# Ten of twelve products in Strassen form, and branch outputs kept in HBM

## The chip, the cores and the metric

The kernel runs on one core of a Trainium2 chip. The metric is the device time of one execution in microseconds (us). The kernel before took 1085.91 us, the median of three runs (1085.72 to 1088.47).

## The reference

One layer on a sequence of 1024 tokens with 1024 channels, all in float32:

```python
h = rmsnorm(x, norm_g)
u_a, v_a, z_a, x_b, c_b, b_b, z_b, g_a, g_b = split(h @ w_in, 9 segments of 1024)
u, v = gelu(u_a), rmsnorm(gelu(v_a), v_norm_g)
y_a = u * (tril(w_s[g]) @ v per 128-token chunk and group + b[g]) * silu(z_a)
y_b = b_b * causal_conv3(c_b * x_b) * silu(z_b)
merged = sigmoid(g_a) * (y_a @ w_branch_a) + sigmoid(g_b) * (y_b @ w_branch_b)
out = rmsnorm(x + merged @ w_out, final_norm_g)
```

There are twelve products of 1024 by 1024 by 1024: nine projections of h, one for each branch (called pa and pb), and the output projection (po).

## The kernel before

Each float32 operand is split into a high and a low part: ScalarE casts the value to the high part and VectorE subtracts it from the value for the low part (`split`, L67 to L69). One float32 product of a 128-row step is then three matmuls into the same PSUM bank, high with high, low with high, high with low (`mm`, L71 to L74). The transposed activations h stay in SBUF for the whole kernel (hT), as two parts of 4 MB.

`block` computes 128 output channels for all 1024 tokens: two halves of 512 tokens, eight steps over the contraction, three matmuls each, 48 matmuls of 128x512 in all. Its weights are one DMA of 512 KB (L265), one cast and one subtraction of 128x1024. A product is eight such blocks, 384 matmuls.

The stages follow each other: a start written out by hand (norm and transposes of x, L112 to L125), v with tokens on partitions, in two halves of 512 channels; branch A, per group of 128 channels the blocks pu and pz and the spatial matmuls pm (L298); gate ga and product pa by turns; branch B, per group the blocks pbc, pbx, pbb, pbz; gate gb and product pb by turns; and the output projection po with the final norm. Results of branches, gates and merged sums stay in SBUF, in 28 slots of 4 KB per partition.

Outside the start, a scheduler fixes the order of each engine's instructions at build time; on the chip each engine runs its list in that order. All loads are on SyncE's queue (SP), also in that order: a DMA there that waits for a semaphore holds back those behind it. A DMA also waits for the earlier one on its completion counter, of which there are eight (DMAHW0 to DMAHW7 in the listings).

Of the kernel before, what the change touches and what calls it, by code (L numbers as in the profile page):

```python
# [19 lines left out]
def hybrid_block(ctx: ExitStack, tc: tile.TileContext, x, norm_g, w_in, v_norm_g, w_spatial,  # L20
# [50 lines left out]
    def mm(acc, a, b, k, nk):  # L71
        """acc += a.T @ b to float32's accuracy; a and b are (high, low) parts."""
        for n, (i, j) in enumerate(((0, 0), (1, 0), (0, 1))):
            nc.tensor.matmul(acc, a[i], b[j], start=k == 0 and n == 0, stop=k == nk - 1 and n == 2)  # L74

    def row_bcast(name, ap):
        t = slot(name)
        nc.sync.dma_start(t, ap.to_broadcast([P, D]))
        return t

    hT = (hpool.tile([P, KT, S], F32R, tag="hT_hi", name="hT_hi"),
          hpool.tile([P, KT, S], F32R, tag="hT_lo", name="hT_lo"))
# [8 lines left out]
    def load_rows(w, k, c0, name):
        raw = wraw.tile([P, D], F32, tag="raw", name=name + "_raw")
        nc.sync.dma_start(raw, w[k * P:(k + 1) * P, c0:c0 + D])
        hl = pair(name)
        split(hl[0], hl[1], raw)
        return hl

    def load_half_rows(w, k, c0, name):
        """Rows k and k+1 (in 128s) of 512 columns."""
        raw = wraw.tile([P, 2, NH], F32, tag="raw", name=name + "_raw")  # L100
        nc.sync.dma_start(raw, w[k * P:(k + 2) * P, c0:c0 + NH].rearrange("(j p) e -> p j e", p=P))
        return raw

    def split_half_rows(raw, name):
        hi, lo = (t.rearrange("p (j e) -> p j e", j=2) for t in pair(name))
        split(hi, lo, raw)
        return [(hi[:, j, :], lo[:, j, :]) for j in range(2)]
# [17 lines left out]
    def v_mm(i, pv, w, k0, k1):  # L125
        ts_ = slice(i * P, (i + 1) * P)
        for k in range(k0, k1):
            mm(pv, [h[:, k, ts_] for h in hT], w[k], k, KT)

    def v_norm(i, vt):  # L130
        sq = small.tile([P, D], BF16, tag="junk", name=f"vsq{i}", bufs=1)
        ss = small.tile([P, 1], F32, tag="ss", name=f"vss{i}")
        nc.scalar.activation(sq, vt, AF.Square, accum_out=ss)
        r = rsqrt_mean([ss], f"rv{i}")
        for g in range(G):
            gs = slice(g * P, (g + 1) * P)
            nc.vector.scalar_tensor_tensor(vg[g][:, i * P:(i + 1) * P], vt[:, gs], r, gv_bc[:, gs],
                                           ALU.mult, ALU.mult)
# [292 lines left out]
```

## Time and profile before

| | before |
|---|---|
| median of three runs | 1085.91 us |
| span of the profiled execution | 1084.3 us |
| TensorE busy | 1075.3 us (99%) |
| VectorE busy | 320.5 us (30%) |
| ScalarE busy | 247.6 us (23%) |
| GpSimd busy | 27.5 us (3%) |
| read from HBM, written | 60.83 MB, 4.19 MB |

A profile is one execution. Its span is measured from the first to the last event of the core; it is 1.6 us below the median. The chain of waits goes back from the last instruction to what released it at each step. A row of the chain or the timeline is: start in us, duration in us, engine, names (tiles) and line. A row of an engine's instructions by line has busy us and the mean ns of one behind the bar, then the idle time ahead of them and what ended it.

### The profile page before, as it was taken

The page shows a single profiled execution, that of the slowest core. Times are in us where ns is not written, and L with a number is a line of the kernel's source. Part 1 is how long each engine was busy: PE and PEld are TensorE (multiplying, and loading weights), DVE is VectorE, ACT ScalarE, POOL GpSimd, SP SyncE. Part 2 cuts the span into 40 slices and gives each one's busy share as a digit, 9 for nine tenths or more (in the row PEclk, how much of TensorE's full clock was granted, in tenths as well). Part 3 has the DMA queues.
Part 4 walks back from the last instruction along what each step waited for, and adds up shares of the span by engine and source line. Part 5 has one row for each costly group of instructions (what it writes and reads, how often), then busy time and mean ns, then how long its engine had stood idle before and what let it go on. Part 6 is the DMA issues. An engine that isn't in the chain of part 4 may idle for free.

```text
span 1084.3 us, 11075 instructions
## 1 busy us (share of the span) xinstructions
PE 1075.3 (99%) x4850; PEld 892.1 (82%) x4850; DVE 320.5 (30%) x354; ACT 247.6 (23%) x297; POOL 27.5 (3%) x69
## 2 busy tenths in 40 slices
PE   8999999999999999999999999999999999999997
PEld 6888888888888888888888888888888888888886
DVE  5543322223311121113323233133231222138322
ACT  5533223323211111112120211111203111134212
POOL 3111000000000000000000000000000000000101
PEclk9999999999999999999999999999999999999999
DMA  7031111111111212121212121212121211114322
GB/s 291 27 106 44 39 39 39 54 44 39 49 49 40 59 39 59 39 59 39 59 39 59 39 59 40 59 39 59 39 59 39 59 40 58 39 59 155 111 84 78
DMA packets 92838, 65.74 MB, mean 61 GB/s; under 512 B 2141, under 2 KB 85109, under 8 KB 92790
## 3 DMA queue, kind: packets, MB, share of 16 engines
q1 hardware_dynamic: 91638, 62.94, 18.8%
q10 hardware_dynamic: 1152, 2.10, 0.7%
q8 instruction: 38, 0.62, 0.2%
q14 instruction: 10, 0.08, 0.0%
HBM read 60.83 MB, written 4.19 MB: 60 GB/s over the span
## 4 chain that ended last, share of the span: by engine, by line
PE 98%; DVE 1%; DMA 1%; ACT 0%; issue 0%; POOL 0%; SPq 0%; POOLq 0%; DVEq 0%; ACTq 0%
PE po L74 8%; PE pu L74 8%; PE pga L74 8%; PE pb L74 8%; PE pgb L74 8%; PE pbz L74 8%; PE pbb L74 8%; PE pbc L74 8%; PE pa L74 8%; PE pz L74 8%; PE pbx L74 8%; PE pv L74 7%; PE pm L298 1%; DMA xt<-in_x_dram 1%; PE xp L122 1%; DVE wv_lo L162 0%
## 5 line engine op out<-in xcount | busy, mean ns | idle before, releaser
L74 PE MATMUL po<-wo_hi,mT_lo 128*128 128x512 f32 (+1 forms) x136 | 51.2, 377 | 0.0
L74 PE MATMUL po<-wo_lo,mT_hi 128*128 128x512 f32 (+1 forms) x136 | 51.2, 376 | 0.0
L74 PE MATMUL po<-wo_hi,mT_hi 128*128 128x512 f32 (+1 forms) x136 | 51.2, 376 | 0.0
L74 PE MATMUL pu<-hT_hi,pu_hi 128*128 128x512 f32 x128 | 50.4, 394 | 0.0
L74 PE MATMUL pga<-hT_hi,pga_hi 128*128 128x512 f32 x128 | 49.9, 390 | 0.0
L74 PE MATMUL pu<-hT_hi,pu_lo 128*128 128x512 f32 x128 | 49.8, 389 | 0.0
L74 PE MATMUL pu<-hT_lo,pu_hi 128*128 128x512 f32 x128 | 49.8, 389 | 0.0
L74 PE MATMUL pga<-hT_hi,pga_lo 128*128 128x512 f32 x128 | 49.8, 389 | 0.0
L74 PE MATMUL pga<-hT_lo,pga_hi 128*128 128x512 f32 x128 | 49.8, 389 | 0.0
L74 PE MATMUL pz<-hT_hi,pz_hi 128*128 128x512 f32 x128 | 49.8, 389 | 0.0
L74 PE MATMUL pz<-hT_hi,pz_lo 128*128 128x512 f32 x128 | 49.8, 389 | 0.0
L74 PE MATMUL pz<-hT_lo,pz_hi 128*128 128x512 f32 x128 | 49.8, 389 | 0.0
L74 PE MATMUL pa<-ya_hi,pa_hi 128*128 128x512 f32 x128 | 49.8, 389 | 0.0
L74 PE MATMUL pa<-ya_hi,pa_lo 128*128 128x512 f32 x128 | 49.8, 389 | 0.0
L74 PE MATMUL pa<-ya_lo,pa_hi 128*128 128x512 f32 x128 | 49.8, 389 | 0.0
L74 PE MATMUL pbc<-hT_hi,pbc_hi 128*128 128x512 f32 x128 | 49.8, 389 | 0.0
L74 PE MATMUL pbc<-hT_hi,pbc_lo 128*128 128x512 f32 x128 | 49.8, 389 | 0.0
L74 PE MATMUL pbc<-hT_lo,pbc_hi 128*128 128x512 f32 x128 | 49.8, 389 | 0.0
L74 PE MATMUL pbx<-hT_hi,pbx_hi 128*128 128x512 f32 x128 | 49.8, 389 | 0.0
L74 PE MATMUL pbx<-hT_hi,pbx_lo 128*128 128x512 f32 x128 | 49.8, 389 | 0.0
L74 PE MATMUL pbx<-hT_lo,pbx_hi 128*128 128x512 f32 x128 | 49.8, 389 | 0.0
L74 PE MATMUL pbb<-hT_hi,pbb_hi 128*128 128x512 f32 x128 | 49.8, 389 | 0.0
(217 smaller groups left out, 2239.7 us busy)
## 6 DMA issues: line engine op xcount, KB each, us to landing
xt<-in_x_dram SPq DMA_DIRECT2D x15, 512.0 KB, 6.5
wv_raw<-in_w_in_dram SPq DMA_DIRECT2D x8, 512.0 KB, 7.9
pu_raw<-in_w_in_dram SPq DMA_DIRECT2D x8, 512.0 KB, 3.6
pz_raw<-in_w_in_dram SPq DMA_DIRECT2D x8, 512.0 KB, 3.6
pga_raw<-in_w_in_dram SPq DMA_DIRECT2D x8, 512.0 KB, 3.6
pa_raw<-in_w_branch_a_dram SPq DMA_DIRECT2D x8, 512.0 KB, 3.9
pbc_raw<-in_w_in_dram SPq DMA_DIRECT2D x8, 512.0 KB, 3.6
pbx_raw<-in_w_in_dram SPq DMA_DIRECT2D x8, 512.0 KB, 3.6
```

The source lines that it names most:

```text
L74: nc.tensor.matmul(acc, a[i], b[j], start=k == 0 and n == 0, stop=k == nk - 1 and n == 2)
L122: nc.tensor.transpose(pt[:, k * P:(k + 1) * P], xt[:, ds_], ident)
L298: nc.tensor.matmul(pm[:, ns], vg[g][:, ns], wsT[:, g * P:(g + 1) * P], start=True, stop=True)
```

## The change

Ten of the twelve products (all but v and the output projection) go in Strassen's form as Winograd arranged it. `step` computes two blocks of 128 output channels at a time, which lie 512 channels apart, for all tokens. Both operands are seen as two by two blocks of halves; eight products of halves become seven, each four steps over the contraction of 512 tokens, so 12 matmuls. A step is 84 matmuls, and there are four steps for each product, 40 in all. The sums of blocks of h (T1 to T4) are made once, and those of weights (S1 to S4) in each step, by VectorE. The seven products accumulate in three PSUM banks (px, pe, pz): products 1, 3, 5 and 7 all add to px, and between them ScalarE copies or VectorE adds the running sum into the result tile C. The last partial sum stays in px.

- Tiles: 20 tiles of 8 KB per partition (`big`), 10 of 4 KB (`page`), two for raw loads (`rawt`); 8 PSUM banks of 512.
- h is kept as four blocks of halves instead of hT. VectorE copies each transposed tile once more from PSUM, and that copy goes to HBM (h_d); `h_blocks` loads halves back in v's second half and makes T1, T2, T4, T3 from them through the two raw tiles.
- v goes to HBM (v_d) without its norm; branch A loads it per group and multiplies the norm in (L437).
- Branch B now comes ahead of branch A, then all of ga, all of gb, then all of pa, and all of pb. What a branch gives goes to HBM as seven blocks, the sums among them (`keep_y`), and is loaded and split again as operand of pa or pb (`y_blocks`). Gates (g_d), the product pa times its gate (ta_d), and the merged sums (m_d) pass through HBM too.
- The output projection loads m per tile of 128 tokens and splits it there. The last pb block is no longer done by halves of the tokens.

```diff
-    NSLOT = 28
+    HP = KT // 2
...
-    hpool = ctx.enter_context(tc.tile_pool(name="hpool", bufs=1))
-    wraw = ctx.enter_context(tc.tile_pool(name="wraw", bufs=3))
-    wspl = ctx.enter_context(tc.tile_pool(name="wspl", bufs=2))
-    slots = ctx.enter_context(tc.tile_pool(name="slots", bufs=NSLOT))
-    ps = ctx.enter_context(tc.tile_pool(name="ps", bufs=3, space=bass.MemoryType.PSUM))
-    ps1 = ctx.enter_context(tc.tile_pool(name="ps1", bufs=2, space=bass.MemoryType.PSUM))
...
+    tp = ctx.enter_context(tc.tile_pool(name="tp", bufs=20))
+    pp = ctx.enter_context(tc.tile_pool(name="pp", bufs=10))
+    rp = ctx.enter_context(tc.tile_pool(name="rp", bufs=2))
+    ps = ctx.enter_context(tc.tile_pool(name="ps", bufs=8, space=bass.MemoryType.PSUM))
+    dp = ctx.enter_context(tc.tile_pool(name="dp", bufs=1, space=bass.MemoryType.DRAM))
...
-    def transpose_x(i, xt, bank=psum1):
-        ts_ = slice(i * P, (i + 1) * P)
-        for k0 in range(0, KT, 4):
...
+    def transpose_x(i, xt):
+        cs = slice(i % 4 * P, (i % 4 + 1) * P)
+        st = page(f"hst{i}").rearrange("p (k t) -> p k t", k=KT)
+        for kh in range(2):
...
-            split(hT[0][:, k0:k0 + 4, ts_], hT[1][:, k0:k0 + 4, ts_], pt.rearrange("p (k t) -> p k t", k=4))
...
+            src = block4(pt)
+            hi, lo = B[kh][i // 4]
+            split(hi[:, :, cs], lo[:, :, cs], src)
+            nc.vector.tensor_copy(st[:, kh * HP:(kh + 1) * HP, :], src)
+        nc.sync.dma_start(h_d[:, :, i * P:(i + 1) * P], st)
...
+    def v_out(i, h, pv):
+        vt = page(f"v{h}_{i}")[:, :NH]
+        nc.scalar.activation(vt, pv, AF.Gelu)
+        sq = small.tile([P, NH], BF16, tag="junk", name=f"vsq{h}_{i}", bufs=1)
+        nc.scalar.activation(sq, vt, AF.Square, accum_out=vss[:, 2 * i + h:2 * i + h + 1])
+        nc.sync.dma_start(v_d[i * P:(i + 1) * P, halves[h]], vt)
...
+    def h_raw(kh, th):
+        t = block4(rawt(f"h{kh}{th}"))
+        nc.sync.dma_start(t, h_d[:, kh * HP:(kh + 1) * HP, halves[th]])
...
+    def h_blocks(n):
+        if n == 0:
+            a, b = h_raw(0, 0), h_raw(0, 1)
+            tt_halves(a, b, a, ALU.subtract)
+            T["T1"] = t_block("T1", a)
+            c = h_raw(1, 1)
+            tt_halves(a, c, a, ALU.subtract)
+            T["T2"] = t_block("T2", a)
+            d = h_raw(1, 0)
+            tt_halves(d, d, a, ALU.subtract)
+            T["T4"] = t_block("T4", d)
+        else:
+            a, b = h_raw(1, 1), h_raw(0, 1)
+            tt_halves(a, a, b, ALU.subtract)
+            T["T3"] = t_block("T3", a)
...
+        if i == 1:
+            h_blocks(0)
+        if i == 4:
+            h_blocks(1)
...
+    def weights(w, c0, name):
+        raw = rawt(name + "_raw").rearrange("p (b k e) -> p b k e", b=2, k=KT)
+        for b in range(2):
+            nc.sync.dma_start(raw[:, b], w[:, c0 + b * NH:c0 + b * NH + P].rearrange("(k p) e -> p k e", p=P))
...
+        w_["A11"], w_["A12"] = parts("a", raw[:, 0])
+        a22 = page(name + "_a22", F32R).rearrange("p (b k e) -> p b k e", b=2, k=HP)
+        split(a22[:, 0], a22[:, 1], raw[:, 1, HP:])
+        w_["A22"] = [a22[:, 0], a22[:, 1]]
+        tt = nc.vector.tensor_tensor
+        s2, s4, s3, s1 = raw[:, 0, :HP], raw[:, 0, HP:], raw[:, 1, :HP], raw[:, 1, HP:]
+        tt(s1, s3, s1, ALU.add)
+        tt(s3, s2, s3, ALU.subtract)
+        tt(s2, s1, s2, ALU.subtract)
+        tt(s4, s4, s2, ALU.subtract)
+        w_["S3"], w_["S1"] = parts("sh", raw[:, 1])
+        w_["S2"], w_["S4"] = parts("sg", raw[:, 0])
+        return w_
+    def product(bank, a, b, start, check=True):
+        for k in range(HP):
+            mm(bank, [t[:, k, :] for t in a], [t[:, k, :] for t in b], start and k == 0, k == HP - 1, check)
+    def step(w, c0, T, name):
+        w_ = weights(w, c0, name)
+        C = big(name).rearrange("p (b t) -> p b t", b=2)
+        lo, hi = halves
+        px, pe, pz = psum(name + "_x"), psum(name + "_e"), psum(name + "_z")
+        add = lambda o, a: nc.vector.tensor_tensor(o, a, o, ALU.add)
+        product(px, w_["A11"], T["B11"], True)
+        nc.scalar.copy(C[:, 0, lo], px)
+        product(pe, w_["S1"], T["T1"], True)
+        nc.scalar.copy(C[:, 1, hi], pe)
+        product(px, w_["S2"], T["T2"], False, False)
+        nc.scalar.copy(C[:, 0, hi], px)
+        product(pz, w_["A12"], T["B21"], True)
+        add(C[:, 0, lo], pz)
+        product(px, w_["S3"], T["T3"], False, False)
+        add(C[:, 1, hi], px)
+        product(pe, w_["S4"], T["B22"], False, False)
+        add(C[:, 0, hi], pe)
+        product(px, w_["A22"], T["T4"], False, False)
+        return C, px
...
+    def activate(C, px, fn):
+        nc.scalar.activation(C[:, 1, halves[0]], px, fn)
+        nc.scalar.activation(C[:, 1, halves[1]], C[:, 1, halves[1]], fn)
+        nc.scalar.activation(C[:, 0], C[:, 0], fn)
+    def times(o, C, px, b):
+        tt = nc.vector.tensor_tensor
+        tt(o[:, 1, halves[0]], px, b[:, 1, halves[0]], ALU.mult)
+        tt(o[:, 1, halves[1]], C[:, 1, halves[1]], b[:, 1, halves[1]], ALU.mult)
+        tt(o[:, 0], C[:, 0], b[:, 0], ALU.mult)
...
+    def keep_y(n, g, y, t):
+        t = t.rearrange("p b (h t) -> p (b h) t", h=2)
+        lo, hi = halves
+        tt = nc.vector.tensor_tensor
+        tt(t[:, 0], y[:, 0, hi], y[:, 0, lo], ALU.subtract)
+        tt(t[:, 1], y[:, 1, hi], t[:, 0], ALU.subtract)
+        tt(t[:, 2], y[:, 1, lo], t[:, 1], ALU.subtract)
+        tt(t[:, 3], y[:, 1, hi], y[:, 0, hi], ALU.subtract)
+        nc.sync.dma_start(y_d[n][:, g, 0, :], y[:, 0, lo])
+        nc.sync.dma_start(y_d[n][:, g, 1:3, :], y[:, 1].rearrange("p (h t) -> p h t", h=2))
+        nc.sync.dma_start(y_d[n][:, g, 3:7, :], t)
+    def y_blocks(n):
+        T = {}
+        for b in ("B11", "T1", "T2", "B21", "T3", "B22", "T4"):
+            raw = block4(big(f"y{n}{b}"))
+            for js in (slice(0, 2), slice(2, 4)):
+                nc.sync.dma_start(raw[:, js, :], y_d[n][:, js, BLOCKS.index(b), :])
+            T[b] = t_block(f"y{n}{b}", raw)
+        return T
...
+    for g in range(HP):
+        c, px = proj("bc", g)
+        nc.scalar.copy(c[:, 1, halves[0]], px)
+        xx, px = proj("bx", g)
+        times(c, xx, px, c)
+        for b in range(2):
+            col = lambda k: cwT[:, k * G + g + b * HP:k * G + g + b * HP + 1]
+            nc.scalar.mul(xx[:, b], c[:, b], col(2))
+            for t in (1, 2):
+                nc.vector.scalar_tensor_tensor(xx[:, b, t:], c[:, b, :S - t], col(2 - t), xx[:, b, t:],
+                                               ALU.mult, ALU.add)
+        bb, px = proj("bb", g)
+        times(xx, bb, px, xx)
+        z, px = proj("bz", g)
+        activate(z, px, AF.Silu)
+        nc.vector.tensor_tensor(xx, xx, z, ALU.mult)
+        keep_y("b", g, xx, z)
...
-    def block(w, c0, rhs, name):
-        hi, lo = block_weights(w, c0, name)
-        po = psum(name)
-        for t0 in range(0, S, NH):
-            for k in range(KT):
-                mm(po[:, t0:t0 + NH], (hi[:, k, :], lo[:, k, :]), [r[:, t0:t0 + NH] for r in rhs[k]], k, KT)
-        return po
...
+    for g in range(HP):
+        u, px = proj("u", g)
+        activate(u, px, AF.Gelu)
+        v = big(f"va{g}").rearrange("p (b n c) -> p b n c", b=2, n=NT)
+        for b in range(2):
+            c0 = g * P + b * NH
+            nc.sync.dma_start(v[:, b], v_d[:, c0:c0 + P].rearrange("(n p) c -> p n c", p=P))
+            nc.vector.tensor_tensor(v[:, b], v[:, b], rv.unsqueeze(2).to_broadcast([P, NT, P]), ALU.mult)
+        z, px = proj("z", g)
+        activate(z, px, AF.Silu)
         nc.vector.tensor_tensor(u, u, z, ALU.mult)
...
+        for b in range(2):
+            gg_ = g + b * HP
...
+            for h in range(2):
+                pm = psum(f"pm{g}{b}{h}")
+                for n in range(HP):
+                    nc.tensor.matmul(pm[:, n * P:(n + 1) * P], v[:, b, h * HP + n], wsT[:, gg_ * P:(gg_ + 1) * P],
+                                     start=True, stop=True)
...
         nc.vector.tensor_tensor(u, u, z, ALU.mult)
...
+        keep_y("a", g, u, z)
...
+    g_d = {n: dram(f"g{n}_d", [P, HP, 2, S]) for n in "ab"}
+    for n in "ab":
+        for g in range(HP):
+            C, px = proj("g" + n, g)
+            activate(C, px, AF.Sigmoid)
+            nc.sync.dma_start(g_d[n][:, g], C)
...
+    ta_d = dram("ta_d", [P, HP, 2, S])
+    m_d = dram("m_d", [P, 2, HP, S])
+    Ta = y_blocks("a")
+    for g in range(HP):
+        C, px = step(w_branch_a[0], g * P, Ta, f"pa{g}")
+        sg = load2(g_d["a"][:, g], f"sga{g}")
+        times(C, C, px, sg)
+        nc.sync.dma_start(ta_d[:, g], C)
+    Tb = y_blocks("b")
+    for g in range(HP):
+        C, px = step(w_branch_b[0], g * P, Tb, f"pb{g}")
+        sg = load2(g_d["b"][:, g], f"sgb{g}")
+        ta = load2(ta_d[:, g], f"ta{g}")
+        times(C, C, px, sg)
+        nc.vector.tensor_tensor(C, C, ta, ALU.add)
+        nc.sync.dma_start(m_d[:, :, g, :], C)
...
-    mT = (hpool.tile([P, KT, S], F32R, tag="hT_hi", name="mT_hi"),
-          hpool.tile([P, KT, S], F32R, tag="hT_lo", name="mT_lo"))
...
-        nc.vector.tensor_tensor(sgs[d][:, cs], pb, sgs[d][:, cs], ALU.mult)
-        nc.vector.tensor_tensor(tb[d][:, cs], tb[d][:, cs], sgs[d][:, cs], ALU.add)
-        split(mT[0][:, d, cs], mT[1][:, d, cs], tb[d][:, cs])
...
+    for k in range(0, KT, 2):
+        raw = rawt(f"wo{k}_raw").rearrange("p (j e) -> p j e", j=2)
+        hi, lo = (big(f"wo{k}_{n}", F32R).rearrange("p (j e) -> p j e", j=2) for n in ("hi", "lo"))
+        for j in range(2):
+            nc.sync.dma_start(raw[:, j], w_out[0, (k + j) * P:(k + j + 1) * P, :])
+            split(hi[:, j], lo[:, j], raw[:, j])
+            wok.append((hi[:, j], lo[:, j]))
...
+        mr = page(f"m{i}").rearrange("p (k t) -> p k t", k=KT)
+        nc.sync.dma_start(mr, m_d[:, :, :, ts_].rearrange("p b k t -> p (b k) t"))
+        mT = [page(f"m{i}_{n}", F32R).rearrange("p (k t) -> p k t", k=KT) for n in ("hi", "lo")]
+        split(mT[0], mT[1], mr)
+        xx = big(f"xo{i}")
+        xt, xf = xx[:, :D], xx[:, D:]
+        nc.sync.dma_start(xt, x[0, ts_, :])
```

How the engines' lists change, at three places. VectorE, from the z product of a group of branch A on; pu and pz are the steps of this group and the next, u and z the same before, `va` is v loaded back, numbers tell tiles apart. Before, at the last group:

```order
L294 TENSOR_TENSOR u_1908<-u_1908,z_1965 128x1024
L69 TENSOR_TENSOR pa_lo<-pa_raw,pa_hi 128x1024
L300 TENSOR_TENSOR z_1965<-pm_1968,b_bc 128x1024
L302 TENSOR_TENSOR u_1908<-u_1908,z_1965 128x1024
L69 TENSOR_TENSOR ya_lo<-u_1908,ya_hi 128x1024
L69 TENSOR_TENSOR pga_lo<-pga_raw,pga_hi 128x1024
```

Now, from the last product of branch A's values of a group to the running sum of the next group's pu:

```order
L452 TENSOR_TENSOR pu_2954<-pu_2954,pz_3078 128x2048
L320 TENSOR_TENSOR pz_raw<-pz_raw 128x512
L379 TENSOR_TENSOR pz_3078<-pu_2954 128x512
L382 TENSOR_TENSOR pz_3078<-pu_2954 128x512
L380 TENSOR_TENSOR pz_3078<-pu_2954,pz_3078 128x512
L437 TENSOR_TENSOR va_3327<-va_3327,rv 128x1024
L381 TENSOR_TENSOR pz_3078<-pu_2954,pz_3078 128x512
L437 TENSOR_TENSOR va_3327<-va_3327,rv 128x1024
L321 TENSOR_TENSOR pz_raw<-pz_raw 128x512
L338 TENSOR_TENSOR pu_3230<-pu_z,pu_3230 128x512
L322 TENSOR_TENSOR pz_raw<-pz_raw 128x512
L74 TENSOR_TENSOR pz_shlo<-pz_raw,pz_shhi 128x1024
```

The sums for the blocks (L379 to L382), v's norm (L437) and the weights' sums (L320 to L322) have come ahead of the additions from PSUM of the next step (L338).

SyncE's queue where the last product starts. Before, pb's weights go by turns with the gate's:

```order
L265 DMA pgb_raw<-in_w_in_dram 128x8x128 [waits DMAHW4_49,DVE_49]
L265 DMA pb_raw<-in_w_branch_b_dram 128x8x128 [waits DMAHW5_49,DVE_49]
L265 DMA pgb_raw<-in_w_in_dram 128x8x128 [waits DMAHW6_49,DVE_49]
L265 DMA pb_raw<-in_w_branch_b_dram 128x8x128 [waits DMAHW7_49,DVE_49]
```

Now, at the end of pa (ybB and ybT are the blocks of branch B's output):

```order
L392 DMA ybT_5560<-yb_d 128x2x512 [waits DMAHW5_49,PE_49]
L392 DMA ybT_5560<-yb_d 128x2x512 [waits DMAHW6_49]
L305 DMA pb_raw<-in_w_branch_b_dram 128x8x128 [waits DMAHW7_49,DVE_49]
L305 DMA pb_raw<-in_w_branch_b_dram 128x8x128 [waits DMAHW0_49]
L476 DMA ta_d<-pa_5451 128x2048 [waits DMAHW1_49,DVE_49]
L392 DMA ybT_5569<-yb_d 128x2x512 [waits DMAHW2_49,PE_49]
L392 DMA ybT_5569<-yb_d 128x2x512 [waits DMAHW3_49]
L392 DMA ybB_5578<-yb_d 128x2x512 [waits DMAHW4_49,PE_49]
L392 DMA ybB_5578<-yb_d 128x2x512 [waits DMAHW5_49]
```

The store of the last pa result, which waits for VectorE, has come ahead of the loads of five of the seven blocks of yb.

SyncE's queue where the output projection starts. Before, only weights, the norm's vector and x are loaded there:

```order
L93 DMA wo_raw<-in_w_out_dram 128x1024 [waits DMAHW2_49,DVE_49]
L78 DMA fg_bc<-in_final_norm_g_dram 128x1024 [waits PE_49]
L88 DMA xt_5752<-in_x_dram 128x1024 [waits PE_49]
L88 DMA xt_5825<-in_x_dram 128x1024 [waits DVE_49]
L402 DMA out_dram<-xt_5752 128x512 [waits DMAHW7_49,DVE_49]
```

Now:

```order
L496 DMA fg_bc<-in_final_norm_g_dram 128x1024 [waits PE_49]
L484 DMA m_d<-pb_6011 256x1x1024 [waits DMAHW2_49,DVE_49]
L505 DMA xo_6158<-in_x_dram 128x1024 [waits DMAHW3_49]
L505 DMA xo_6236<-in_x_dram 128x1024 [waits DMAHW4_49,PE_49]
L500 DMA m_6152<-m_d 128x8x128 [waits DMAHW5_49,DMAHW2_49]
```

The store of the last merged sums and the load of m's first tile, which waits for that store to land (DMAHW2), now stand between pb and the output projection.

## Rows read from the trace of the kernel before

**Rows 1.** The page: span and busy time of each engine

```profile
span 1084.3 us, 11075 instructions
PE 1075.3 (99%) x4850; PEld 892.1 (82%) x4850; DVE 320.5 (30%) x354; ACT 247.6 (23%) x297; POOL 27.5 (3%) x69
```

**Rows 2.** The page: TensorE's clock in 40 slices; the chain's shares by engine

```profile
PEclk9999999999999999999999999999999999999999
...
PE 98%; DVE 1%; DMA 1%; ACT 0%; issue 0%; POOL 0%; SPq 0%; POOLq 0%; DVEq 0%; ACTq 0%
```

**Rows 3.** The chain of waits in time order, pieces from each stage

```profile
12.83 3.35 DVE wv_lo L162 x2
16.18 1.20 DVE hT_lo L69 x2
17.38 1.21 DVE g_bc L209 x2
18.78 1.30 DVE xt L114
20.12 1.09 PE xp L122 x8
21.21 5.50 PE pv L74 x24
...
127.65 1.78 PE pm L298 x16
...
468.45 10.88 PE pbc L74 x48
...
968.93 21.76 PE pb L74 x96
990.69 87.36 PE po L74 x408
1078.08 0.44 DVE xt L392
```

**Rows 4.** VectorE's instructions by line and shape

```profile
L396 DVE TENSOR_TENSOR xf<-xt,fg_bc 128x512 f32<-128x512 f32 x15 | 10.4, 692 | 0.5
L328 DVE SCALAR_TENSOR_TENSOR cv<-c,cwT,cv 128x1023 f32<-128x1023 f32 x8 | 10.3, 1284 | 0.3
L335 DVE TENSOR_TENSOR cv<-cv,bz 128x1024 f32<-128x1024 f32 x8 | 9.8, 1225 | 76.7 <-ACT bz L334 76.7
```

**Rows 5.** ScalarE's instructions by line and shape

```profile
L293 ACT ACT_TABLE_LOAD x8 | 10.3, 1283 | 0.1
L68 ACT CAST pbc_hi<-pbc_raw 128x1024 fp32r<-128x1024 f32 x8 | 8.4, 1053 | 68.8 <-PE pbb L74 68.8
L311 ACT ACTIVATE sga<-pga 128x1024 f32<-128x1024 f32 x8 | 8.2, 1029 | 73.2 <-PE pga L74 73.2
L251 ACT ACTIVATE vt<-pv 128x512 f32<-128x512 f32 x8 | 4.8, 598 | 25.9 <-PE pv L74 25.8
```

**Rows 6.** The page: DMA issues, KB each, us to landing

```profile
pbc_raw<-in_w_in_dram SPq DMA_DIRECT2D x8, 512.0 KB, 3.6
...
out_dram<-xt SPq DMA_DIRECT2D x8, 256.0 KB, 2.2
```

**Rows 7.** What the DMA engines moved from 8 to 11 us

```profile
DMA packets 629, 1.22 MB, mean 408 GB/s; under 512 B 33, under 2 KB 33, under 8 KB 629
```

**Rows 8.** Busy time and granted clock in stretches at the kernel's end

```profile
core 0: us, PE busy (x) PEld busy (x) DVE busy (x) ACT busy (x) POOL busy (x), PEclk, DMA share, GB/s
1076.00:1078.00 2.00, 2.00 (x18) 1.83 (x16) 0.09 (x1) 0.23 (x2) 0.27 (x1) 1.00 0.00 0
1078.00:1079.00 1.00, 0.04 (x1) 0.00 (x0) 0.85 (x2) 0.40 (x2) 0.00 (x0) 1.00 0.00 0
...
1082.00:1083.00 1.00, 0.00 (x0) 0.00 (x0) 0.00 (x0) 0.00 (x0) 0.00 (x0) 0.94 0.93 356
1083.00:1084.20 1.20, 0.00 (x0) 0.00 (x0) 0.00 (x0) 0.00 (x0) 0.00 (x0) 0.50 0.00 0
```

More of the change, by code (lines that the diff above doesn't have):

```diff
@@ L69, in split, with mm, block4 @@
         nc.vector.tensor_tensor(lo, src, hi.bitcast(F32), ALU.subtract)
-    def mm(acc, a, b, k, nk):
+    def mm(acc, a, b, start, stop, check=True):
         for n, (i, j) in enumerate(((0, 0), (1, 0), (0, 1))):
[L74 to L82, printed above, removed]
-    wv = w_in[0]
+            nc.tensor.matmul(acc, a[i], b[j], start=start and n == 0, stop=stop and n == 2,
+                             skip_group_check=not check)
+    def block4(t):
+        return t.rearrange("p (k t) -> p k t", k=HP)
+    wv = w_in[0]
+    B = [[tuple(block4(big(f"h{kh}{th}_{n}", F32R)) for n in ("hi", "lo")) for th in range(2)]
+         for kh in range(2)]
+    h_d = dram("h_d", [P, KT, S])
+    v_d = dram("v_d", [S, D])
+    vss = const.tile([P, 2 * NT], F32, name="vss")
+    rv = const.tile([P, NT], F32, name="rv")
+    x2 = {}
     def load_x(i):
-        xt = slot(f"xt{i}")
+        if i // 2 not in x2:
+            x2[i // 2] = big(f"x{i // 2}")
+        xt = x2[i // 2][:, (i % 2) * D:(i % 2 + 1) * D]
         nc.sync.dma_start(xt, x[0, i * P:(i + 1) * P, :])
         return xt
[L91 to L107, printed above, removed]
     def norm_x(i, xt, g):
@@ L125, in v_mm @@
[L125 to L138, printed above, removed]
@@ L145, in hybrid_block @@
+    gg = big("gg")
+    g_row, g_bc = gg[:, :D], gg[:, D:]
+    ones = const.tile([P, P], F32, name="ones")
     with tc.manual_schedule(engines={ET.SP, ET.PE, ET.Activation, ET.DVE, ET.Pool}):
-        g_row = slot("g_row")
         nc.vector.memset(g_row, 0.0)
-        ones = slot("ones")[:, :P]
         nc.gpsimd.memset(ones, 1.0)
+        x2[0], x2[1] = big("x0"), big("x1")
+        xs = [x2[i // 2][:, (i % 2) * D:(i % 2 + 1) * D] for i in range(4)]
         for cs in halves:
@@ L170, in hybrid_block @@
             nc.sync.dma_start(xs[i], x[0, i * P:(i + 1) * P, :])
-        pg = [psum1(f"g_ps{h}") for h in range(2)]
+        pg = [psum(f"g_ps{h}") for h in range(2)]
         def keep_warm(n):
@@ L210, in hybrid_block, with v_mm @@
         norm_x(2, xs[2], g_bc)
-    vts, w1 = [], []
+    def v_mm(i, pv, w, k0, k1):
+        for k in range(k0, k1):
+            mm(pv, hk(i, k), w[k], k == 0, k == KT - 1)
+    w1 = []
     with tc.manual_schedule(engines={ET.SP, ET.Activation, ET.DVE}):
@@ new lines, in hybrid_block @@
+            if i in (4, 6):
+                k = 2 * (i - 4)
+                raw = block4(rawt(f"wv1{i}_raw"))
+                hi, lo = (block4(big(f"wv1{i}_{n}", F32R)) for n in ("hi", "lo"))
+                nc.sync.dma_start(raw, wv[k * P:(k + 4) * P, D + NH:2 * D].rearrange("(j p) e -> p j e", p=P))
+                w1 += [(hi[:, j, :], lo[:, j, :]) for j in range(4)]
+            if i >= 4:
+                js = slice(2 * (i % 2), 2 * (i % 2) + 2)
+                split(hi[:, js, :], lo[:, js, :], raw[:, js, :])
@@ new lines, in hybrid_block, with t_block @@
+    cw = const.tile([4 * G, P], F32, name="cw")
+    nc.sync.dma_start(cw[:3 * G, :], conv_w[0].rearrange("k (g p) -> (k g) p", p=P))
+    nc.sync.dma_start(cw[3 * G:, :], v_norm_g[0].rearrange("(g p) -> g p", p=P))
+    cwT = const.tile([P, 4 * G], F32, name="cwT")
+    def t_block(name, raw):
+        hi, lo = (block4(big(f"{name}_{n}", F32R)) for n in ("hi", "lo"))
+        for js in (slice(0, 2), slice(2, 4)):
+            split(hi[:, js, :], lo[:, js, :], raw[:, js, :])
+        return hi, lo
@@ new lines, in proj @@
+    def proj(seg, g):
+        return step(wv, SEG[seg] * D + g * P, T, f"p{seg}{g}")
+    BLOCKS = ["B11", "B21", "B22", "T1", "T2", "T4", "T3"]
+    y_d = {n: dram(f"y{n}_d", [P, HP, 7, NH]) for n in "ab"}
+    def keep_y(n, g, y, t):
[9 more added lines that the diff above has]
+        nc.sync.dma_start(y_d[n][:, g, 3:7, :], t)
@@ L240, in hybrid_block @@
+    cst = big("cst")
+    wsT, b_bc = cst[:, :D], cst[:, D:]
+    ws = page("ws")
     nc.sync.dma_start(ws.rearrange("t (g s) -> t g s", g=G), w_spatial[0].rearrange("g t s -> t g s"))
```

219 lines of the change are left out of this document (75 added, 144 removed).

## The prediction

> **What bounds the kernel now.** The page comes first: TensorE is busy for 1075.3 of 1084.3 us, VectorE for 30%, ScalarE for 23% [rows 1], and the granted clock is full in all slices [rows 2]. The chain of waits is TensorE for 98%, so before TensorE's first long stretch and behind its last there is little else [rows 2]. In order of time the chain shows three stages: the start, where norm and transposes hold TensorE until 20.12, then unbroken blocks, one of 48 matmuls per 10.88 us, then 87.36 us of output projection, which ends at 1078.05, and a tail of some 6 us [rows 3]. So a matmul of 128x512 costs 10.88 / 48 = 0.2267 us (twice the block, 96 in 21.76, gives the same), and the time is their number plus what TensorE waits. A change is priced here in two columns: matmuls taken away, and waits added to an engine that has none.
>
> **What is removed.** Ten products fall from 384 to 40 x 84 / 10 = 336 matmuls: 10 x 48 = 480 fewer. They lie on the bounding engine one behind the other, so 480 x 0.2267 = 108.8 us go. With no new wait the span would be 1084.3 - 108.8 = 975.5. pm's matmuls stay (1.78 us a group [rows 3]).
>
> **What is added, and whether something covers it.** Prices first. VectorE, back to back: 1.23 for 1024 columns, 0.69 for 512, 1.28 for a convolution step [rows 4]. ScalarE: 1.05 for a cast of 1024, 0.60 for 512 out of PSUM, 1.03 for an activation of 1024, 1.28 for a table [rows 5]. DMA: 512 KB land after 3.6 us, a store of 256 KB after 2.2 [rows 6], and beyond that a loaded system moves 408 GB/s [rows 7], so each further 512 KB adds 0.52 / 0.408 = 1.3: a load of 1 MB is some 4.9, a store of 1 MB some 2.2 + 0.79 / 0.408 = 4.1.
>
> *A step in the steady state.* A product of halves is 12 x 0.2267 = 2.72 us, a step 84 x 0.2267 = 19.04. VectorE has in it 3.5 splits (4.3), four sums of 512 (2.8) and three additions from PSUM (2.1), 9.2 in all; pbx adds 2.6 of gating and 4 x 1.28 of convolution, 16.9. ScalarE has 3.5 casts and three copies, 5.5, and up to 3.5 for activations. Both fit under 19.04. A copy of px may last until the product after the next begins, one product of slack (2.72), and takes 0.60. So in branch B and the gates I take 0; if VectorE were late there, each step would pay the lateness, which is the slower rival below.
>
> *Start.* Two copies of 512 from PSUM per transposed tile (L180 of the new kernel) stand on VectorE. Those of the first two tiles come ahead of the norm of the third, which TensorE awaits: the chain runs 12.83, 16.18, 17.38, 18.78, 20.12 on VectorE alone [rows 3]. Four copies at 0.60 to 0.69 are 2.4 to 2.8: +2.7. Later tiles' copies are hidden under 5.46 us of v.
>
> *From v to the first step.* With only two raw tiles, each of the loads for T1, T2, T4, T3 waits until VectorE is done with an earlier one. Counted from the beginning of v's second half: the second half of h lands at 9.7 (behind the split of v's last weights, 4.7, plus a load of 4.9), its subtraction takes 2.4, and three further links of load and subtraction with a split between bring T3's operands to 36.9, its subtraction to 39.2, and the first step's weights to 43.6. v itself ends at 8 x 24 x 0.2267 = 43.5, and the cast stands on ScalarE behind v's last gelu (0.60) and square; cast and subtraction end at 46.5 or a little later. So +3.6; 1 if the links are shorter than the rows, 10 if each load takes two more.
>
> *Branch A.* After z's last product VectorE has activation-bound work that goes out in a row: u times z (2.4), four additions for pm (2.8), u again (2.4), then, as the list shows, sums for the blocks, v's norm and the weights' sums ahead of the next group's additions from PSUM. I count 18.6 to 20.5 us until the addition of px of the next pu is done. TensorE wants that bank again for product 7, at 6 x 2.72 + 1.78 = 18.1. So 0.5 to 2.4 in each of three groups: +3, between 0 and 9.
>
> *Where pa begins.* The seven blocks of ya need tiles that the last gate step gives back one by one, and the store of gate gb's last tile, which waits for ScalarE, is ahead of some of their loads. The list interleaves products of the next pa step, which hides most; two waits stay, 1.1 for a page of weights and 2.8 for T2's cast. With 0.4 for the issue ahead: +4.3, between 0 and 12.
>
> *Where pb begins.* No such filling is left. The store of the last pa tile waits until VectorE has multiplied px, 1.0 behind TensorE's last pa matmul; behind it on SyncE stand T2, then B21. Store, T2 and B21 are 3 MB, at 408 GB/s 7.7 us, with the landing some 10 behind pa's end; with the split about 11.1. TensorE reaches B21 after two products, at 5.44. 5.7 idle, and 2.8 again for T2's operand later, with 0.8 for the queue: +9.3, between 4 and 18.
>
> *Where the output projection begins.* Before, the last pb went by halves and m stayed in SBUF; TensorE went from pb to po with no gap [rows 3]. Now the last product must be multiplied and added, four instructions until 4.4 behind pb's end; the store of 1 MB takes 4.1 (8.5), m's first tile 3.6 and queueing (12.7), the cast 1.05 and the subtraction 1.23: TensorE starts about 15 behind. Nothing else is left to fill this. +15, between 10 and 22.
>
> *Clock.* [...] Between 0 and 10 for three such places; I take 4, one and a half products. [...]
>
> *Sum.* 2.7 + 3.6 + 3 + 4.3 + 9.3 + 15 + 4 = 41.9. 1084.3 - 108.8 + 41.9 = 1017.4 of span; with the 1.6 between this profile's span and the median, 1019.
>
> **Rivals.**
>
> 1. *The waits are mostly hidden.* The scheduler's order, pools and queues could let blocks arrive in time; for it speaks that DMA is nearly idle through most of the kernel. Against: at the end nothing can cover the round trip. Start 2.7 and end 10 alone: 975.5 + 12.7 + 1.6 = 990.
> 2. *The round trips cost twice as much.* Loads that queue on eight completion counters and one in-order queue can be late by one another; tiles of 8 KB are few. All waits but the start doubled: 975.5 + 2.7 + 78.4 + 1.6 = 1058.
> 3. *Slower: each step's chain through PSUM stalls.* Products 3, 5, 7 go on in px only after a copy or an addition has read it. If the reader on ScalarE or VectorE comes a whole product late once in each step, because it stands behind splits of the next weights in its list, that is 40 x 2.72 = 109, the whole saving, and with the 41.9 the time is 1019 + 109 = 1128. It decides from (1085.9 - 1019) / 40 = 1.7 us of stall per step on. For it: the lists put splits (1.23 each) between the additions, and three to four in a row use up the 2.72. Against: VectorE's 9.2 and ScalarE's 5.5 to 9 leave half of a step free. [...]
>
> That the matmuls aren't removed is no rival: the new list has 480 fewer of 128x512.
>
> **How the numbers follow.** My forecast, each transition paying about what I counted, gets 0.60 (1003 to 1040); hidden waits 0.14; dear round trips 0.18 (up to 1060, and a tail of 0.02 to 1083); stalls in each step 0.06; what ends near the old time 0.02. The likeliest is 1019. The range goes from rival 1's 988 to 1060. Runs differ by 0.3%, 3.3 us, which is what a measurement can tell: faster 0.92, within it 0.02, slower 0.06.
>
> **What would show it.** In the profile after: TensorE busy about 967 (1075.3 - 108.8, plus lower clock); steps of 19.04 without gaps in branch B; first v transposes some 2.7 later; a gap of 2 to 5 before the first pbc; 9 in pb's first step; 15 between pb and po, with store and load of m in the chain, and PEclk below full there. Wrong I'd be if idle time lies inside all steps, put down to VectorE's additions or ScalarE's copies; or if the gaps at the three transitions are absent.

## The result and the profile after

The changed kernel took 1036.38 us (median of four runs, 1034.98 to 1037.39) against 1087.19 of the kernel before in the same session: a ratio of 0.9532, 95% interval 0.9517 to 0.9547. It is faster, by 51 us where 67 were forecast, and 1036.4 lies between 988 and 1060. The profiled execution has a span of 1035.7 and took 1037.39.

The page after has these rows for [rows 1, 2]: span and busy times, the granted clock in 40 slices, the chain's shares by engine.

```profile
span 1035.7 us, 11024 instructions
PE 981.4 (95%) x4370; PEld 808.0 (78%) x4370; DVE 628.3 (61%) x732; ACT 400.6 (39%) x548; POOL 32.0 (3%) x77
...
PEclk9989899999999999999999999999999989997999
...
PE 82%; DMA 10%; DVE 3%; ACT 3%; issue 1%; SPq 1%; POOLq 0%; POOL 0%; DVEq 0%; ACTq 0%
```

The instruction counts show the 480 matmuls gone (4850 to 4370). TensorE's busy time fell by 93.9, not by 108.8: the difference, 14.9, is work done more slowly, and the clock row now has slices below 9 near both ends. Its idle time rose from 9.0 to 54.3, by 45.3. Together 60.2, which is 1035.7 - 975.5: the waits, where 41.9 were forecast. Cut at the borders of the stages (columns as in [rows 8]) it looks like this: start, v in two pieces, branch B, branch A, gates, pa, pb, the gap, the output projection.

```profile
0.00:23.37 23.37, 18.66 (x75) 13.83 (x76) 13.28 (x18) 13.53 (x21) 8.09 (x17) 0.93 0.70 249
23.37:77.00 53.63, 47.60 (x220) 38.63 (x217) 23.40 (x31) 22.34 (x43) 4.26 (x13) 0.94 0.59 175
77.00:124.13 47.13, 40.07 (x175) 32.30 (x175) 21.59 (x20) 20.80 (x37) 8.17 (x19) 0.97 0.60 187
124.13:431.40 307.27, 306.80 (x1346) 253.54 (x1347) 203.44 (x239) 111.26 (x142) 2.31 (x3) 0.99 0.27 81
431.40:598.98 167.58, 167.58 (x810) 141.38 (x809) 119.03 (x138) 72.14 (x91) 0.00 (x0) 1.00 0.41 126
598.98:751.30 152.32, 152.32 (x674) 126.15 (x673) 84.45 (x101) 64.98 (x84) 0.00 (x0) 1.00 0.39 131
751.30:840.44 89.14, 84.74 (x361) 67.92 (x359) 61.98 (x72) 35.29 (x44) 0.00 (x0) 0.98 0.65 229
840.44:923.70 83.26, 73.55 (x312) 59.46 (x312) 58.94 (x63) 32.19 (x38) 0.00 (x0) 0.96 0.74 267
923.70:939.10 15.40, 0.00 (x1) 0.01 (x1) 6.61 (x7) 3.13 (x3) 0.00 (x0) 0.61 0.79 277
939.10:1029.24 90.14, 90.09 (x408) 74.74 (x408) 34.25 (x47) 23.68 (x46) 8.37 (x23) 0.97 0.33 108
```

Branch B, branch A and the gates have no idle TensorE after the first step, although VectorE is busy for two thirds of branch B. The idle time lies elsewhere: at the start, in v and ahead of the first step, in the first steps of pa and of pb, and ahead of the output projection. What TensorE waited for, from the list of waits (who waited, whom it waited for, total us, times, longest):

```profile
PE po L79 <- ACT m_hi L73: 15.4, 1, 15.4
PE pb_z L79 <- ACT ybB_hi L73: 7.3, 1, 7.3
PE pbc_x L79 <- ACT pbc_ahi L73: 6.9, 1, 6.9
PE pv L79 <- ACT h_hi L73: 5.1, 1, 5.1
PE pv L200 <- ACT h_hi L73: 2.7, 1, 2.7
PE pb_x L79 <- ACT pb L340: 2.4, 1, 2.4
PE pa_x L79 <- ACT pa L340: 2.3, 1, 2.3
```

The list names the cast on ScalarE that came last. The chain in order of time says what held that cast, here at the start, in v and at the first step:

```profile
19.75 3.63 PE pv L79 x16
23.37 0.45 PE xp L118 x4
...
46.12 0.33 SPq L134
...
46.54 8.43 DMA wv_raw<-in_w_in_dram
...
55.94 1.06 ACT h_hi L73 x2
...
69.06 6.97 DMA wv_raw<-in_w_in_dram
...
79.32 1.24 DVE wv_lo L74
...
80.57 6.00 DMA h<-h_d
...
89.08 5.70 DMA h<-h_d
...
97.27 5.72 DMA h<-h_d
...
107.75 8.90 DMA h<-h_d
...
119.13 3.88 DMA pbc_raw<-in_w_in_dram
...
125.39 4.11 PE pbc_x L79 x11
```

The wait of 5.1 in v is not in the forecast. SyncE issues the load of v's next weights (46.54) only behind the store of v's tile (L134), which waits for ScalarE's gelu. ScalarE's next instruction is the cast of those weights, so it stands until 54.99, and the cast of the next tile of h (55.94), which TensorE awaits, stands behind it. The gelu had itself waited 1.4 us for the store before it to land; what that is worth was not tried.

Farther down are the links of load and subtraction that were forecast, each load longer than forecast (5.7 to 8.9 instead of 4.9). The first of these loads begins at 80.57, when VectorE has split the last of v's weights (79.32) and so given back their raw tile: 8.4 us behind the beginning of v's second half (72.16), where 4.7 were counted. The first step's weights land at 123.01, 50.9 behind that beginning, where 43.6 were counted.

The clock behind the gap at the end, and behind a short stop in pa's first step (the column before the last two is the granted clock):

```profile
770.00:772.00 2.00, 0.58 (x3) 0.16 (x1) 0.53 (x1) 1.61 (x2) 0.00 (x0) 1.00 1.06 442
772.00:773.00 1.00, 0.08 (x1) 0.08 (x1) 1.00 (x2) 1.00 (x3) 0.00 (x0) 1.00 0.24 98
773.00:776.00 3.00, 3.00 (x8) 2.37 (x9) 3.00 (x4) 2.27 (x4) 0.00 (x0) 0.56 0.68 199
...
927.00:939.00 12.00, 0.00 (x0) 0.00 (x0) 3.29 (x3) 1.00 (x1) 0.00 (x0) 0.50 0.84 286
939.00:944.00 5.00, 4.87 (x11) 3.38 (x12) 1.74 (x2) 1.09 (x2) 0.00 (x0) 0.50 1.07 363
944.00:945.00 1.00, 1.00 (x6) 0.83 (x5) 0.71 (x1) 0.00 (x0) 0.00 (x0) 0.99 1.13 322
```

After 15.4 us idle the granted clock is 0.50 when the output projection begins, and stays there for 5 us of work (939 to 944). A stop of 2.3 us (770.6 to 772.9) is followed by a lower clock as well, 0.56 over 3 us. Busy time times (1 - clock), summed over single microseconds, gives 3.0 us lost behind the stop in v, 1.8 in the first step, 1.7 in pa, 2.1 in pb, 2.4 in the output projection: 11.0, and 1.7 at the start. The other 2.2 of the 14.9 lie in pa's and pb's matmuls (below).

### The profile page after: what moved, and what is told of

Its sections match the earlier page's. It is cut to its first block, busy times and chain, and to the rows that moved or that the text cites. A ratio compares the mean times of both kernels' runs of the same rounds, so it can differ in the third digit from the quotient of the medians.

```text
span 1035.7 us, 11024 instructions
## 1 busy us (share of the span) xinstructions
PE 981.4 (95%) x4370; PEld 808.0 (78%) x4370; DVE 628.3 (61%) x732; ACT 400.6 (39%) x548; POOL 32.0 (3%) x77
## 4 chain that ended last, share of the span: by engine, by line
PE 82%; DMA 10%; DVE 3%; ACT 3%; issue 1%; SPq 1%; POOLq 0%; POOL 0%; DVEq 0%; ACTq 0%
PE po L79 9%; PE pbc_x L79 4%; PE pu_x L79 4%; PE pga_x L79 4%; PE pbz_x L79 4%; PE pz_x L79 4%; PE pbb_x L79 4%; PE pbx_x L79 4%; PE pgb_x L79 4%; PE pb_x L79 3%; PE pa_x L79 3%; DMA h<-h_d 3%; PE pbc_e L79 2%; PE pga_e L79 2%; PE pz_e L79 2%; PE pu_e L79 2%
## 5 line engine op out<-in xcount | busy, mean ns | idle before, releaser
L79 PE MATMUL po<-wo_hi,m_hi 128*128 128x512 f32 (+1 forms) x136 | 52.2, 385 | 15.4 <-ACT m_hi L73 15.4
L79 PE MATMUL pv<-wv_hi,h_hi 128*128 128x512 f32 x120 | 48.7, 406 | 5.6 <-ACT h_hi L73 5.1
L79 PE MATMUL po<-wo_hi,m_lo 128*128 128x512 f32 (+1 forms) x136 | 52.1, 383 | 0.0
L79 PE MATMUL po<-wo_lo,m_hi 128*128 128x512 f32 (+1 forms) x136 | 51.9, 382 | 0.0
L79 PE MATMUL pv<-wv_hi,h_lo 128*128 128x512 f32 x120 | 47.8, 401 | 0.6 <-DVE h_lo L74 0.6
L79 PE MATMUL pv<-wv_lo,h_hi 128*128 128x512 f32 x120 | 47.7, 399 | 0.0
L79 PEld LDWEIGHTS po<-wo_hi,m_hi 128*128 128x128 f32 x136 | 26.1, 193 | 20.6 <-ACT m_hi L73 15.8
L79 PEld LDWEIGHTS pv<-wv_hi,h_hi 128*128 128x128 f32 x120 | 23.2, 193 | 11.3 <-ACT h_hi L73 5.5
L79 PEld LDWEIGHTS po<-wo_hi,m_lo 128*128 128x128 f32 x136 | 26.0, 191 | 5.6 <-DVE m_lo L74 0.8
L79 PEld LDWEIGHTS po<-wo_lo,m_hi 128*128 128x128 f32 x136 | 26.0, 191 | 4.8
L74 DVE TENSOR_TENSOR h_lo<-xp,h_hi 128x512 fp32r<-128x512 f32 x16 | 11.0, 685 | 15.4 <-ACT h_hi L73 15.4
L338 DVE TENSOR_TENSOR pbz<-pbz_z,pbz 128x512 f32<-128x512 f32 x4 | 2.8, 692 | 28.6 <-PE pbz_z L79 28.6
L338 DVE TENSOR_TENSOR pz<-pz_z,pz 128x512 f32<-128x512 f32 x4 | 2.8, 691 | 24.9 <-PE pz_z L79 24.9
L338 DVE TENSOR_TENSOR pbx<-pbx_z,pbx 128x512 f32<-128x512 f32 x4 | 2.8, 692 | 24.9 <-PE pbx_z L79 24.9
```

What stands on the lines that cost most here:

```text
L74: nc.vector.tensor_tensor(lo, src, hi.bitcast(F32), ALU.subtract)
L79: nc.tensor.matmul(acc, a[i], b[j], start=start and n == 0, stop=stop and n == 2, skip_group_check=not check)
L338: add = lambda o, a: nc.vector.tensor_tensor(o, a, o, ALU.add)
```

## The experiments

Each run is set against the changed kernel's 1036.4; differences between sessions of the kernel before were under 0.5 us (1087.2 to 1087.6).

**Weights of v's second half loaded early.** The two loads go to the loop's second and third pass, the splits stay.

```diff
...
+            if i in (1, 2):
+                k = 4 * (i - 1)
+                raw1.append(block4(rawt(f"wv1{i}_raw")))
+                nc.sync.dma_start(raw1[-1], wv[k * P:(k + 4) * P, D + NH:2 * D].rearrange(...))
...
-                raw = block4(rawt(f"wv1{i}_raw"))
-                nc.sync.dma_start(raw, wv[k * P:(k + 4) * P, D + NH:2 * D].rearrange(...))
+                raw = raw1[k // 4]
```

> The loads of the weights of v's second half are issued in the loop's second and third pass instead of its fifth and seventh; all else as in the changed kernel (1036.4). Theory (SyncE's order: these loads stood behind v's store, which waits for ScalarE, and ScalarE then waits for the load ahead of a tile's cast): the idle 5.1 + 0.6 + 0.5 us in v and the 3.3 us of lower clock behind it go, some 9.5 in all, about 1027; the gap of 6.9 ahead of the first Strassen step stays. Rival (the blocks T1 to T4 set the pace of the whole stage): the first step begins no earlier, its gap grows by what v gains, time within 2 us of 1036.

1022.8 us, ratio 0.9409 (0.9395 to 0.9423): 13.6 less. No idle stretch of v is left in its trace, which confirms SyncE's order as the cause. The gap ahead of the first step shrank too, from 6.9 to 1.6, which neither theory expected: the chain for T1 to T4 also waited for a raw tile that these late weights held (79.32 and 80.57 above). What stays there, by this run's chain, is the cast of the step's weights behind v's last gelu.

```profile
PE pbc_x L79 <- ACT pbc_ahi L73: 1.6, 1, 1.6
```

**T1 to T4 made in 4 KB tiles.** The raw tiles are left to weights.

```diff
     def h_raw(kh, th):
-        t = block4(rawt(f"h{kh}{th}"))
-        nc.sync.dma_start(t, h_d[:, kh * HP:(kh + 1) * HP, halves[th]])
+        t = [page(f"h{kh}{th}{n}").rearrange("p (k t) -> p k t", k=2) for n in range(2)]
+        for n in range(2):
+            nc.sync.dma_start(t[n], h_d[:, kh * HP + 2 * n:kh * HP + 2 * n + 2, halves[th]])
         return t
...
```

> The halves of h that T1, T2, T4 and T3 are made of are loaded into eight tiles of 4 KB instead of the two raw tiles, and the raw tiles are left to weights. Theory (two raw tiles make load, subtraction and load a serial chain): the four loads overlap, the first step's weights come early, the gap of 6.9 + 0.5 us ahead of the first step and the 2.2 us of lower clock behind it go: about 1027. Rival (no chain of tiles but the queue, the 4 KB tiles come free as late): the gap shrinks by less than 2 us, 1034 to 1037.

1030.6 us, ratio 0.9488 (0.9472 to 0.9504): 5.8 less; the gap fell from 6.9 + 0.5 to 1.6 + 0.8. The chain through the raw tiles was the cause of 5.0 us of the gap. The 5.8 are 3.6 less than the 9.4 expected: 2.4 of idle time stayed, the cast and subtraction behind v's last gelu, and so did a stretch of lower clock behind it (1.7).

**Stores of gates and pa by GpSimd.**

```diff
-            nc.sync.dma_start(g_d[n][:, g], C)
+            nc.gpsimd.dma_start(g_d[n][:, g], C)
...
-        nc.sync.dma_start(ta_d[:, g], C)
+        nc.gpsimd.dma_start(ta_d[:, g], C)
```

> The stores of gates (g_d) and of pa times its gate (ta_d) are issued by GpSimd instead of SyncE, so that no load of a block of ya or yb stands behind one that waits for ScalarE or VectorE. Theory (queueing): of the 7.3 us gap in pb's first step 5 or more go with the lower clock behind it (2.2), and 1 of the 4.4 us in pa's: 1027 to 1030. Rival (the tiles come free too late, or the loads themselves take the 9 us): the gap stays within 2 us, 1034 to 1037.

1038.9 us, ratio 0.9559 (0.9545 to 0.9573): nothing gained, and above both expectations. The gap in pb is 6.2 instead of 7.3; the waits in pa's first step are 6.4 instead of 4.4, with two stretches of lower clock instead of one, which was not followed up. For pb, SyncE's longest wait and its issues (start, us) show why. In the changed kernel:

```profile
SPq L305 <- DVE pb_sglo L74: 12.9, 1, 12.9
...
834.20 1.00 SPq L305 DMA_DIRECT2D pb_raw<-in_w_branch_b_dram  x2
835.93 0.34 SPq L476 DMA_DIRECT2D ta_d<-pa  x1
836.37 0.89 SPq L392 DMA_DIRECT2D ybT<-yb_d  x2
837.36 3.30 SPq L392 DMA_DIRECT2D ybB<-yb_d  x2
```

In this run:

```profile
835.08 0.37 SPq L305 DMA_DIRECT2D pb_raw<-in_w_branch_b_dram  x1
835.55 1.04 SPq L392 DMA_DIRECT2D ybT<-yb_d  x2
836.64 0.46 SPq L305 DMA_DIRECT2D pb_raw<-in_w_branch_b_dram  x1
837.21 1.77 SPq L392 DMA_DIRECT2D ybB<-yb_d  x2
```

The next pb step's weights (L305) stand ahead of the store and wait for a raw tile, which the split of the weights before them gives back: until 834.20 in the changed kernel, until 835.07 here. The store (L476) had held the queue for only 0.7 us more, from 835.20 to 835.93. The loads of T2 and B21 begin at 835.55 and 837.21, nearly as before (836.37 and 837.36). So taking away this one wait doesn't tell whether the queue or the tiles of the blocks set the time.

**Loads of ya and yb by GpSimd.** That tells it apart: now the loads have a queue of their own.

```diff
-                nc.sync.dma_start(raw[:, js, :], y_d[n][:, js, BLOCKS.index(b), :])
+                nc.gpsimd.dma_start(raw[:, js, :], y_d[n][:, js, BLOCKS.index(b), :])
```

> All loads of the blocks of ya and yb are issued by GpSimd instead of SyncE; the stores stay on SyncE. In the run with the stores moved, a load of weights that waited for a raw tile took the store's place ahead of yb's loads, which began at 835 as before. Theory (what heads SyncE's queue holds the loads): with a queue of their own they begin as each tile comes free, some 5 us sooner; pb's gap falls from 7.3 to 3 or less, its lower clock (2.2) goes, pa's gaps (4.4) shrink by 1 to 2: 1027 to 1031. Rival (the tiles that pa's last step holds, or the 390 GB/s at which the transfers ran from 836 on, set the time): the gap stays within 2 us of 7.3, 1034 to 1038.

1025.6 us, ratio 0.9435 (0.9417 to 0.9453): 10.8 less, somewhat more than the theory had. GpSimd issues T2's two loads at 816.80 and 821.25 and B21's at 822.75 and 824.01, 13 to 20 us ahead of SyncE before:

```profile
816.80 0.73 POOL L392 DMA_DIRECT2D ybT<-yb_d  x1 [1.51 <-PE pa_e L79]
...
822.75 0.72 POOL L392 DMA_DIRECT2D ybB<-yb_d  x1 [0.78 <-issue]
```

So the tiles were free, and the queue had held the loads. The 7.3 us gap in pb and the waits of 0.9, 0.9 and 0.2 in pa are gone, 9.3 in all; what stays in both is the wait for the copy of px (2.4 and 2.3, as in the list above). The gap ahead of the first Strassen step, which this edit doesn't touch, was 5.5 in this execution instead of 6.9.

**The last merged sums from SBUF.** The last pb tile feeds the output projection directly, which takes the other six blocks of the contraction first.

```diff
-        nc.sync.dma_start(m_d[:, :, g, :], C)
+        if g < HP - 1:
+            nc.sync.dma_start(m_d[:, :, g, :], C)
...
+        split(mT[0][:, HP - 1::HP], mT[1][:, HP - 1::HP], C[:, :, ts_])
...
-            for k in range(KT):
+            for k in (0, 1, 2, 4, 5, 6, 3, 7):
```

> The merged sums of the last pb step are taken from its tile in SBUF instead of going through HBM, and the output projection takes the six other blocks of the contraction first. Theory (the round trip is the gap): TensorE goes from pb to the output projection with 0 to 3 us idle instead of 15.4 and keeps its clock (2.5): 1018 to 1021. Rival (the multiplications, additions and splits behind the last product are the larger part of the gap): 8 us or more of it stay, 1026 to 1031.

1020.6 us, ratio 0.9389 (0.9375 to 0.9403): 15.8 less, as the theory had it. In this run's list the 15.4 has become

```profile
PE po L79 <- DVE m_lo L74: 2.5, 1, 2.5
```

and the granted clock behind it reads 1.00 (931 to 940). The round trip through HBM was the gap.

**TensorE kept busy ahead of the output projection.** First 130, then 160 transposes of the identity, which nothing reads (the edit is shown with 160).

```diff
         product(px, w_["A22"], T["T4"], False, False)
+        if name == "pb3":
+            for _ in range(160):
+                nc.tensor.transpose(pe[:, :P], ident, ident)
```

> The changed kernel with 130 transposes of the identity (0.109 us each, 14 us), which nothing reads, on TensorE between the last pb product and the output projection. Theory (the lower clock is the price of the idle stretch ahead): the output projection begins as late as before but runs at full clock, 87.4 us instead of 90.1, 2 to 3 us less, 1033.5 to 1034.5. Rival (the output projection is slower by its new operands, page by page, not by the clock): it stays at 90, 1036 to 1037.

> As the run with 130 transposes, with 160, 17.4 us, so that nothing of the stretch ahead of the output projection stays idle: there the last 2.4 us were still idle and the clock fell to 0.50 for 7 us behind them. Theory (any break, not its length, costs the clock): the output projection now runs at full clock, 87.4 to 88 us instead of 90.1, and the time is 1033 to 1035. Rival (transposes of 128 columns do not keep the clock, or the projection's own pace is 90): 1036 to 1039.

130: 1038.3 us, ratio 0.9549 (0.9532 to 0.9566), above both expectations, which it doesn't tell apart. The transposes ended at 936.3, TensorE stood for the last 2.4 us, and the clock fell all the same, later: 0.69 from 939 to 940, then

```profile
940.00:946.00 6.00, 6.00 (x14) 4.74 (x15) 1.23 (x1) 1.04 (x1) 0.00 (x0) 0.50 1.08 371
```

160: no stop is left, and the chain reads

```profile
920.61 17.47 PE pb_e L354 x160
938.08 87.53 PE po L79 x408
```

The granted clock reads 1.00 in each microsecond from 918 to 950, and the output projection takes 87.53, as before the change (87.36), instead of 90.14. So 2.6 us are the clock's, and the projection has next to no other loss (0.2). The whole time doesn't show it: 1036.0 us, ratio 0.9535 (0.9510 to 0.9560), with runs from 1033.8 to 1040.4; this reading rests on the trace.

**Several at once.** No new edits; the first is weights early and last sums from SBUF, then ya and yb by GpSimd besides, then T1 to T4 in 4 KB tiles besides.

> v's weights early and the last merged sums from SBUF, both at once. Theory (the waits lie one behind another on TensorE and add up): 1036.4 - 13.6 - 15.8 = 1007. Rival (one wait covers part of another): 1012 or more.

> The same two with the loads of ya and yb issued by GpSimd besides. Theory (queue ahead of yb's loads): 1007 less 5 to 9, 998 to 1002. Rival (tiles or transfer rate): 1006 to 1008.

> The last combination (weights early, last merged sums from SBUF, ya and yb by GpSimd's queue: 997.6) with T1 to T4 made in 4 KB tiles besides. Theory (the chain of load and subtraction through two raw tiles still delays the first step's weights): the 4.2 us idle in the first step go, 992 to 995. Rival (what is left there is the casts of the first step behind v's gelus on ScalarE): 996 to 998.

1006.9 us (0.9259, 0.9240 to 0.9278), 997.6 us (0.9170, 0.9151 to 0.9189) and 996.1 us (0.9156, 0.9135 to 0.9177). The first three savings, 13.6, 15.8 and 10.8, add to 40.2; 1036.4 - 40.2 = 996.2 stands against 997.6. The waits lie one behind another, and none covered another by more than runs of one kernel differ. The 4 KB tiles add nothing measurable once the weights come early: the rival holds, the first step's 1.6 and 0.8 stay, as with the early weights alone.

**Blocks of ya and yb one product ahead of their use.**

```diff
+        def __getitem__(self, b):
+            for c in self.ORDER[:self.ORDER.index(b) + 2]:
+                if c not in self:
...
+                    self[c] = t_block(f"y{self.n}{c}", [raw[:, :2, :], raw[:, 2:, :]])
```

> As the run with all four, and the blocks of ya and yb are loaded and split one product ahead of their use instead of all seven ahead of the first step, so that the copy of px stands ahead of the casts of later blocks on ScalarE. Theory (the 2.3 and 2.4 us ahead of the third product wait for that copy): both go, 4 to 7 us less than that run. Rival (with less of the next step's products between them, TensorE now waits for each block to land): 0 to 10 us more than that run.

995.4 us, ratio 0.9155 (0.9141 to 0.9169), the same as the run before it. The wait for the copy has gone and one for T2's cast has come in the same place, 1.6 + 0.5 instead of 2.3 in either step: neither theory in full, a wait turned into another. This is the lowest median of all, 91.8 us below the kernel before and 41 below the changed one.

## Why the prediction was right, and which steps were off

- *480 matmuls at 0.2267.* Right: steps of 19.04 (152.32 for the eight gate steps) and 480 fewer matmuls.
- *No stall in the steady state.* Right, and with it the slower rival falls: branch B's 16 steps take 307.27 where 16 x 19.04 = 304.6, and 2.3 of the 2.6 are the first step's idle 0.5 and its lower clock, 1.8. The granted clock read 1.00 for all of branch A and the gates, 320 us in which TensorE has no idle time.
- *Start, 2.7.* Measured 3.3 (20.12 to 23.37, [rows 3]), but not for that cause: the norm on VectorE begins at 21.07 instead of 18.78, 2.3 later, as counted, and ends at 22.35, before TensorE comes to its result. TensorE was held to 23.37 by its own work (the chain's first rows): the second tile of x landed 1.1 later (9.46 instead of 8.35), TensorE stood idle for 2.7 us ahead of the first products instead of 0.7, and the lower clock behind that (0.59, 0.50, 0.50 and 0.70 from 12 to 16) took 1.7. That the size came out is luck.
- *From v to the first step, 3.6.* Measured 13.6: 6.9 + 0.5 there and 5.1 + 0.6 + 0.5 within v. This is the step that failed most. (Its own count ends at 46.5, 3.0 behind v's 43.5; the 3.6 stands on the "little later".) The links were priced with unloaded loads (4.9 for 1 MB against 5.7 to 8.9), and SyncE's list was read from v's second half on; that v's stores had come ahead of v's own loads in the first half was not looked at. That order cost the 6.2 within v and 3.7 of the 7.3 by which the first step's weights were late.
- *Branch A, 3.* Measured 0. VectorE's addition of px ended at 488.32, 17.9 behind z's last product, a little sooner than counted; but the term had its deadline from one block's pm, 1.78, where a step has two, 3.56. So the bank was wanted at 19.9, not 18.1.
- *pa, 4.3; pb, 9.3; end, 15.* Measured 4.4, 9.7 and 15.4. pb's step was right in size and only in part in cause: SyncE's queue did hold the loads, but for 12.9 us at the next weights, which waited for a raw tile, and only 0.7 at the store, and moving the store alone gave nothing. The end was right in cause; store and load took 5.2 and 4.6 where 4.1 and 4.2 were counted, and TensorE began behind the cast, without the 1.23 of the subtraction, so that these two errors nearly cancel.
- *Clock, 4.* Measured 11.0 besides the start. No run shows the 4, an estimate of one and a half products for three places. The runs showed 1.7 to 3.0 for one stop of the changed kernel, near one product (2.72), and five stops that paid: in v, at the first step, in pa, in pb and ahead of the output projection; the one of 2.3 us in pa cost 1.7. This step failed too.

The seven add up to 3.3 + 13.6 + 0 + 4.4 + 9.7 + 15.4 + 11.0 = 57.4 of 60.2, where 41.9 were forecast. The two steps that failed are 17.0 too small; branch A's 3, taken and not paid, hide a little of it. Of the other 2.8, some 2.2 lie in pa's and pb's busy time (158.3 for eight steps, less 152.3, less 3.8 of clock); what makes those matmuls longer was not tried. Of the rivals, the waits were neither mostly hidden (1) nor all twice as dear (2): v's and the clock's cost about four and three times what was taken, pa's, pb's and the end's what was counted.
